# Hybrid attention and delta-rule layer: two groups of the triangular substitution side by side during the fourth head, two projection steps among the merges

## The chip, the cores and the metric

The kernel runs on one core of a Trainium2 chip, as one program. The metric is the device time of one execution in microseconds (us). The kernel before was timed in three runs; one more execution was recorded by the hardware profiler, and every line of a profile below comes from it.

## The reference, cut to what matters

The layer mixes 1024 latent tokens and 256 context tokens of width 1024 in two head groups: neighbourhood attention (8 heads) and a gated delta rule run in both directions (4 heads of 128, chunks of 64). The part that the change touches is the chunk's triangular inverse in the delta rule.

```python
    decay = jnp.exp(jnp.where(incl, gc[..., :, None] - gc[..., None, :], -jnp.inf))
    kb = k * beta[..., None]
    a = jnp.where(pos[:, None] > pos[None, :],
                  jnp.einsum('nbhid,nbhjd->nbhij', kb, k) * decay, 0.0)
    eye = jnp.eye(GDN_CHUNK, dtype=a.dtype)
    t_inv = lax.linalg.triangular_solve(eye + a, jnp.broadcast_to(eye, a.shape),
                                        left_side=True, lower=True, unit_diagonal=True)
    u = jnp.einsum('nbhij,nbhje->nbhie', t_inv, v * beta[..., None])
    w = jnp.einsum('nbhij,nbhjd->nbhid', t_inv, kb * jnp.exp(gc)[..., None])
```

The kernel inverts the 32 x 32 diagonal blocks by back substitution and puts the chunk's inverse together from them by small matmuls (the merge).

## The kernel before, in words

The work goes through these stages.

- `phase0` loads and modulates the tokens and starts the first projections.
- `phase2` goes through the four delta heads h = 0 to 3. Each head takes the steps Q, K (projection and short convolution of q and k), then F of the head before (`delta_front`: Gram products `pk`, decay `em`, the matrices `pm` and `qe`), then the steps `R V p p T p p U B`: R is a part of the residual gate (`res_gate`, it ends in the small matmul `pg` behind ScalarE's copy `growg`), V the projection and convolution of v (`acc_v`, `xp_v`), p one step of a filling generator, T the transposes to token order with the norms' squares and the rotary product (`tp`, `tok`, `rot`), U the transposes of v (`vtp`), B the transposes back (`tb`, `kq`).
- The filling generator `projections` has 32 steps; a step is 24 matmuls for one tile of a projection (`pz`, `pq`, `pk`) or 48 shorter ones for two tiles of values (`pv`). 16 of them are taken in `phase2`.
- `phase_a2` takes the other steps and lets two generators run beside them, by credits that each step adds: `blocks` (group 2 of the substitution, then loads for attention) and `merges` (`inv_merge` of the four heads, in the order of the table MERGES: matmuls `tz`, `tu` between copies on ScalarE and VectorE).
- `phase_b` holds attention and the scan of the delta rule, `phase4` the output projection.

The substitution works on 320 blocks of 32 x 32, one in each partition: `delta_front` gathers 80 of a head into `ab_dram`, and groups 0, 1 and 2 hold 120, 120 and 80 of them (`inv_load`). `inv_blocks` clears `vb`, sets its diagonal to 1 on GpSimd, and runs 31 pairs of VectorE instructions, an outer product into `tb` (L1078) and a subtraction from `vb` (L1081). The result goes to `yd`, from which the merges load. Group 0 is spread over the steps of h = 2 and the Q and K of h = 3, group 1 over the steps of h = 3, group 2 runs in `phase_a2`.

The order of the instructions on each engine is fixed when the program is built, by a scheduler that goes by priorities and estimated times; each engine then takes its instructions in that order. SyncE and ScalarE issue the transfers, each in its own order. All names in the rows (`acc_v2`) carry the head's number behind the name.

## Time and profile before

| what | value |
| --- | --- |
| median of 3 runs | 873.86 us (870.09 to 876.51) |
| span of the profiled execution | 869.9 us |
| the profiled execution's own time | not given apart from its span; the lowest timed run is 0.2 us above that span |
| instructions | 16461 |
| TensorE busy | 824.9 us, 95% |
| VectorE busy | 502.7 us, 58% |
| ScalarE busy | 417.3 us, 48% |
| GpSimd busy | 357.3 us, 41% |

The page gives busy time by engine over the span. Since TensorE is busy nearly always, a share over the whole span says little here; the waits of TensorE in each stage and its granted clock say more. In the views PE is TensorE's matmul, PEld its weight load, DVE VectorE, ACT ScalarE, POOL GpSimd, SP SyncE, and a `q` behind an engine means its instruction queue.

### The profile page before, as it was taken

Reading aid. Unit: us, or ns where it says so; the run is one execution under the profiler, and the core shown is the slowest. Engines: PE = TensorE matmul, PEld = TensorE weight load, DVE = VectorE, ACT = ScalarE, POOL = GpSimd, SP = SyncE. Lnnn points to the kernel's source line nnn. Section 1 sums busy time; section 2 is a strip of 40 time slices with the busy share of each in tenths; the row PEclk is TensorE's granted clock in tenths of the full one; section 3 lists DMA queues with packets and bytes.
Section 4 is the critical chain, followed back from the end, with each engine's and each line's share of the span. In section 5 each row is a group of like instructions: output and inputs, shape, how many; then the busy total and the mean of one; then the engine's idle time right before and its main releaser. Section 6 shows DMA issues by size and latency. Waiting matters only on the chain.

```text
span 869.9 us, 16461 instructions
## 1 busy us (share of the span) xinstructions
PE 824.9 (95%) x6082; PEld 696.4 (80%) x6082; DVE 502.7 (58%) x1051; ACT 417.3 (48%) x1087; POOL 357.3 (41%) x430
## 2 busy tenths in 40 slices
PE   6999999999999989989898999899999999999996
PEld 3678887888788867769786788788898988878885
DVE  3444455536743699859935964456666655653342
ACT  5244334753664643355314334366666667734210
POOL 2224141453462553328262100655757559624110
PEclk9999999999999999989998999699999999999999
DMA  8778352255444825562597569995967925134251
GB/s 340 265 259 295 97 170 88 73 170 168 142 157 154 221 85 170 176 171 81 176 283 226 160 187 290 419 258 149 313 179 262 259 78 191 49 110 133 87 184 69
DMA packets 86054, 159.65 MB, mean 184 GB/s; under 512 B 18373, under 2 KB 45334, under 8 KB 83798
## 3 DMA queue, kind: packets, MB, share of 16 engines
q1 hardware_dynamic: 78486, 144.94, 53.0%
q10 hardware_dynamic: 7488, 13.67, 5.1%
q8 instruction: 48, 0.79, 0.4%
q14 instruction: 32, 0.26, 0.1%
HBM read 109.51 MB, written 52.42 MB: 186 GB/s over the span
## 4 chain that ended last, share of the span: by engine, by line
PE 59%; DVE 16%; DMA 15%; issue 4%; ACT 2%; POOL 2%; SPq 1%; DVEq 0%; POOLq 0%; ACTq 0%
PE py L1369 3%; PE py L1370 3%; PE py L1371 3%; DVE tb L1078 3%; DVE vb L1081 3%; PE pa L1260 2%; PE pz L463 2%; PE pz L468 2%; PE pz L467 2%; PE po L789 2%; DMA wada<-in_w_ada 2%; PE pa L1271 2%; PE po L784 2%; DMA pm_dram<-pm 2%; PE tr L772 2%
## 5 line engine op out<-in xcount | busy, mean ns | idle before, releaser
L759 ACT ACTIVATE pt<-pt,nm 128x544 f32<-128x544 f32 (+1 forms) x64 | 50.5, 790 | 37.5 <-DVE nm L758 37.0
L758 DVE CUSTOM_DVE_ANT_0 pt<-sc,gm 128x544 f32<-128x544 f32 (+1 forms) x64 | 49.4, 771 | 32.2 <-PE sc L754 25.8
L742 POOL TENSOR_TENSOR gm<-gt,mk 128x288 f32<-128x288 f32 (+1 forms) x48 | 46.5, 971 | 29.1 <-DVE nm L758 28.8
L1232 POOL TENSOR_SCALAR kd<-kt,kd 128x128 f32<-128x128 f32 x72 | 42.7, 605 | 20.5 <-PE pa L1271 19.9
L1020 ACT ACTIVATE em<-em,gc 128x128 f32<-128x128 f32 x80 | 25.5, 391 | 34.9 <-DMA em<-gc_dram 29.7
L467 PE MATMUL pz<-hl,wh_gz 128*128 128x512 f32 x96 | 38.6, 402 | 0.0
L463 PE MATMUL pz<-hh,wh_gz 128*128 128x512 f32 x96 | 38.3, 399 | 0.0
L468 PE MATMUL pz<-hh,wl_gz 128*128 128x512 f32 x96 | 38.2, 398 | 0.0
L476 PE MATMUL pv<-wh_nv,hh 128*128 128x264 f32 x128 | 35.5, 296 | 2.0 <-ACT hh L265 1.7
L477 PE MATMUL pv<-wh_nv,hl 128*128 128x264 f32 x128 | 36.8, 292 | 0.0
L1431 DVE TENSOR_TENSOR finv<-py,ggb 128x512 f32<-128x512 f32 x16 | 10.9, 689 | 43.2 <-ACT finv L1430 43.1
L478 PE MATMUL pv<-wl_nv,hh 128*128 128x264 f32 x128 | 35.6, 287 | 0.0
L1274 DVE SCALAR_TENSOR_TENSOR s<-s,egl,pa 128x128 f32<-128x128 f32 x64 | 19.6, 344 | 27.2 <-PE pa L1271 27.2
L1039 POOL TENSOR_SCALAR_AFFINE_SELECT qe<-qe 128x256 f32<-128x256 f32 x32 | 25.5, 800 | 24.1 <-DVE qe L1038 24.1
L887 DVE SCALAR_TENSOR_TENSOR acc_v<-xp_v,cols,acc_v 128x1282 f32<-128x1282 f32 x16 | 29.1, 1817 | 10.9 <-ACT acc_v L885 10.6
L1078 DVE TENSOR_TENSOR tb<-ab,vb 120x31 f32<-120x31 f32 (+15 forms) x62 | 30.2, 487 | 8.7 <-DMA ab<-ab_dram 7.1
L1137 POOL COPY tm<-ld 32x320 f32<-32x320 f32 x16 | 7.4, 464 | 65.0 <-DMA tm_dram<-tm 27.1
L1430 ACT ACTIVATE finv<-py 128x512 f32<-128x512 f32 x16 | 9.5, 597 | 48.6 <-PE py L1371 30.5
L1238 POOL TENSOR_SCALAR vb<-v,beta 128x128 f32<-128x128 f32 x40 | 24.2, 604 | 20.4 <-DVE y L1244 17.2
L772 PE MATMUL tr<-c,pt 128*96 128x128 f32 (+1 forms) x192 | 31.8, 275 | 0.0
L1035 DVE SCALAR_TENSOR_TENSOR pm<-pk,beta,em 128x128 f32<-128x128 f32 x80 | 23.5, 342 | 14.0 <-PE pk L1028 10.9
L770 ACT COPY tcx<-tc 128x256 f32<-128x256 f32 x64 | 23.4, 366 | 16.2 <-PE tc L768 15.8
(432 smaller groups left out, 2852.7 us busy)
## 6 DMA issues: line engine op xcount, KB each, us to landing
wada<-in_w_ada SPq DMA_DIRECT2D x16, 512.0 KB
em<-gc_dram SPq DMA_DIRECT2D x20, 256.0 KB
pm_dram<-pm SPq DMA_DIRECT2D x20, 256.0 KB
tm_dram<-tm SPq DMA_DIRECT2D x8, 640.0 KB
kk<-qk_dram SPq DMA_DIRECT2D x16, 320.0 KB
tm<-tm_dram SPq DMA_DIRECT2D x4, 1280.0 KB
kq_dram<-kq SPq DMA_DIRECT2D x4, 1152.0 KB
kq<-kq_dram SPq DMA_DIRECT2D x4, 1152.0 KB
```

The costliest lines, as they stand in the source:

```text
L463: r = nc.tensor.matmul(ps, wh, xh, start=(k == 0), stop=False)
L467: nc.tensor.matmul(ps, wh, xl, start=False, stop=False)
L468: nc.tensor.matmul(ps, wl, xh, start=False, stop=(k == KC - 1))
L476: nc.tensor.matmul(ps, xh, wh, start=(k == 0), stop=False)
L477: nc.tensor.matmul(ps, xl, wh, start=False, stop=False)
L478: nc.tensor.matmul(ps, xh, wl, start=False, stop=(k == KC - 1))
L742: r = nc.gpsimd.tensor_tensor(self.gm[hh][:, 384 - n:384].rearrange("p (n c r) -> p n c r", c=nco, r=4), gv, self.mk[:, mo:mo + n].rearran ...
L758: nc.vector.tensor_tensor_reduce(pt[:, 384 - n:], sc[:, 512 - n:768], gm[:, 384 - n:], -1.0, 3.0e38, ALU.add, ALU.min, nm)
L759: self.last_exp = nc.scalar.activation(pt[:, 384 - n:], pt[:, 384 - n:], AF.Exp, bias=nm, scale=-1.0, accum_out=sums[:, ct, hh:hh + 1]).in ...
L772: self.pe(nc.tensor.transpose(pl[:m, rc * P:(rc + 1) * P], pt[:, 384 + (rc - 3) * m:384 + (rc - 2) * m], self.ident))
L1078: nc.vector.tensor_tensor(t3, bc(ab[:, 0:m, m:m + 1], [r, m, n]), bc(vb[:, m:m + 1, m:], [r, m, n]), ALU.mult)
L1232: r = nc.gpsimd.tensor_scalar(kd[d], kt_[:, t, :], self.kd[:, h, d, t:t + 1], None, ALU.mult)
```

## The change: two groups in one run

Groups 0 and 1 are no longer run one after the other. A new function `inv_pairs` loads both into the halves of one tile of 2 x 1024 columns, cuts away all but the strict triangle on GpSimd, sets the diagonals to 1, and substitutes in place: 30 pairs of VectorE instructions, each over both groups. It starts at h = 3, behind F of head 2; during h = 2 there is no substitution. The sign is moved into `pm` (the factor is now minus beta, kept in `nsc` until the scan needs its own values there), so that the substitution adds and the merges copy where they negated. At h = 2 two of the four `p` are left out, so that 18 instead of 16 steps of the filling generator remain for `phase_a2`, and a step there gives the merges 1.5 credits instead of 3. The gate preparation takes its small tiles as parts of one buffer of the `tok` pool.

```diff
                 step(h - 1, "F") if h else step(h, "G")
-                if h > 1:
-                    blocks = self.inv_groups((h - 2,), lambda nm, n: cv.tile([P, n], F32, name=nm, tag=nm[:2]))
-                for c in "RVppTppUB":
+                if h == 3:
+                    blocks = self.inv_pairs(cv)
+                for c in ("RVppTppUB", "RVppTppUB", "RVpTpUB", "RVppTppUB")[h]:
                     step(h, c)
                     next(blocks, None)
...
+        tmp = vp.tile([P, 512], F32, name="gtmp", tag="tok", bufs=6)
+        part = lambda o: tmp[:, 80 * o:80 * o + 80].rearrange("p (h d t) -> p h d t", h=4, d=2)
...
-        nc.vector.tensor_scalar(fl(self.nsc), fl(self.egc), -1.0, None, ALU.mult)
-        nc.vector.tensor_tensor(self.nsc[:, :, 1, :], self.nsc[:, :, 1, :], beta[:, :, 1, :], ALU.mult)
+        nc.vector.tensor_scalar(fl(self.nsc), fl(beta), -1.0, None, ALU.mult)
...
-                    nc.vector.scalar_tensor_tensor(pm[:, d, t - t0, :], pk[:, t - t0, 0, :], self.beta[:, h, d, t:t + 1],
+                    nc.vector.scalar_tensor_tensor(pm[:, d, t - t0, :], pk[:, t - t0, 0, :], self.nsc[:, h, d, t:t + 1],
                                                    em[:, d, t - t0, :], ALU.mult, ALU.mult)
...
+    def inv_pairs(self, pool):
+        nc = self.nc
+        ab = pool.tile([P, 2 * S], F32, name="ab", tag="ab")
+        tb = pool.tile([P, 480], F32, name="tb", tag="tb")[:120]
+        for g in range(2):
+            w = self.inv_load(g, ab[:, S * g:S * g + S])
+            nc.gpsimd.affine_select(w, w, [[-1, 32], [1, 32]], ALU.is_gt, 0.0, base=0, channel_multiplier=0)
+        ab = ab[:120].rearrange("p (g a b) -> p g a b", g=2, a=32)
+        nc.gpsimd.memset(bass.AP(ab.tensor, ab.offset, [list(ab.ap[0]), [S, 2], [33, 32]]), 1.0)
+        yield
+        for m in range(30, 0, -1):
+            n = 31 - m
+            t3 = tb[:, :2 * m * n].rearrange("p (g a b) -> p g a b", g=2, a=m)
+            nc.vector.tensor_tensor(t3, bc(ab[:, :, 0:m, m:m + 1], [120, 2, m, n]), bc(ab[:, :, m:m + 1, m + 1:], [120, 2, m, n]),
+                                    ALU.mult)
+            nc.vector.tensor_tensor(ab[:, :, 0:m, m + 1:], ab[:, :, 0:m, m + 1:], t3, ALU.add)
+            if m % 3 == 0:
+                yield
+        yield
+        for g in range(2):
+            self.yd[g] = self.dp.tile([120, 32, 32], F32, name=f"yd{g}")
+            nc.sync.dma_start(self.yd[g], ab[:, g])
...
-                nc.vector.tensor_tensor(vb[:, 0:m, m:], vb[:, 0:m, m:], t3, ALU.subtract)
+                nc.vector.tensor_tensor(vb[:, 0:m, m:], vb[:, 0:m, m:], t3, ALU.add)
...
-                nc.vector.tensor_scalar(dst, pu[sc], -1.0, None, ALU.mult)
+                nc.vector.tensor_copy(dst, pu[sc])
...
         if h == 0:
+            fl = lambda t: t.rearrange("p h d t -> p (h d t)")
+            nc.vector.tensor_scalar(fl(self.nsc), fl(self.egc), -1.0, None, ALU.mult)
+            nc.vector.tensor_tensor(self.nsc[:, :, 1, :], self.nsc[:, :, 1, :], self.beta[:, :, 1, :], ALU.mult)
...
-                for i, (g, r) in enumerate(zip(gens, (3, 3))):
+                for i, (g, r) in enumerate(zip(gens, (3, 1.5))):
```

Where this moves instructions is seen in the fixed orders. First VectorE in the third head, at the convolution of v (`acc_v2`), before:

```order
L1078 TENSOR_TENSOR tb0_2755<-ab0_2752,vb0_2754 120x87
L887 SCALAR_TENSOR_TENSOR acc_v2_2769<-xp_v2_2768,cols_62,acc_v2_2769 128x1282
L1081 TENSOR_TENSOR vb0_2754<-vb0_2754,tb0_2755 120x29x3
L529 TENSOR_TENSOR sl_k12_2902<-pk1_2_2876,sh_k12_2901 128x256
L887 SCALAR_TENSOR_TENSOR acc_v2_2769<-xp_v2_2768,cols_62,acc_v2_2769 128x1282
L1078 TENSOR_TENSOR tb0_2755<-ab0_2752,vb0_2754 120x112
```

The same place now:

```order
L887 SCALAR_TENSOR_TENSOR acc_v2_2757<-xp_v2_2756,cols_62,acc_v2_2757 128x1282
L529 TENSOR_TENSOR sl_k12_2884<-pk1_2_2858,sh_k12_2883 128x256
L887 SCALAR_TENSOR_TENSOR acc_v2_2757<-xp_v2_2756,cols_62,acc_v2_2757 128x1282 x3
L529 TENSOR_TENSOR sl_k10_3004<-pk1_0_2978,sh_k10_3003 128x512
L889 SCALAR_TENSOR_TENSOR acc_v2_2757<-xp_v2_2756,acc_v2_2757 128x1282
```

The steps of group 0 between the taps of the convolution are gone. Second GpSimd, where F of head 2 begins (`qe2` is masked there), before:

```order
L449 TENSOR_TENSOR wl_gv3_4_3538<-wr_gv3_4_3536,wh_gv3_4_3537 128x512
L1071 MEMSET vb1_3528 120x1024
L1039 AFFINE_SELECT qe2_2_3418<-qe2_2_3418 128x256
L1072 MEMSET vb1_3528 120x32
L1039 AFFINE_SELECT qe2_2_3418<-qe2_2_3418 128x256
```

And now:

```order
L449 TENSOR_TENSOR wl_gv3_4_3391<-wr_gv3_4_3389,wh_gv3_4_3390 128x512
L1040 AFFINE_SELECT qe2_2_3268<-qe2_2_3268 128x256 x2
L1040 AFFINE_SELECT qe2_4_3290<-qe2_4_3290 128x256 x2
L1040 AFFINE_SELECT qe2_6_3312<-qe2_6_3312 128x256 x2
L1040 AFFINE_SELECT qe2_8_3334<-qe2_8_3334 128x256 x2
```

The clearing of group 1's `vb` no longer stands ahead of the masks. Third VectorE in the fourth head, behind the convolution of v, now (L1080 and L1082 are the two instructions of a pair; `wl_nv0` is the low part of the weights of the value projection, which the matmuls `pv` read):

```order
L889 SCALAR_TENSOR_TENSOR acc_v3_3396<-xp_v3_3395,acc_v3_3396 128x1282
L1080 TENSOR_TENSOR tb_3377<-ab_3376 120x216
L556 SCALAR_TENSOR_TENSOR st_z10_3561<-st_z10_3561,pz1_0_3536 128x512
L1082 TENSOR_TENSOR ab_3376<-ab_3376,tb_3377 120x2x27x4
L1080 TENSOR_TENSOR tb_3377<-ab_3376 120x260
L1082 TENSOR_TENSOR ab_3376<-ab_3376,tb_3377 120x2x26x5
L1080 TENSOR_TENSOR tb_3377<-ab_3376 120x300
L1082 TENSOR_TENSOR ab_3376<-ab_3376,tb_3377 120x2x25x6
L1080 TENSOR_TENSOR tb_3377<-ab_3376 120x336
L1082 TENSOR_TENSOR ab_3376<-ab_3376,tb_3377 120x2x24x7
L449 TENSOR_TENSOR wl_nv0_6_3721<-wr_nv0_6_3719,wh_nv0_6_3720 128x528
```

Before, this weight part stood ahead of the last tap of the convolution, behind six instructions of the substitution. The first tokens `tok3` of the head follow 16 instructions of the pair later.

More of the change, by code (lines that the diff above doesn't have):

```diff
@@ L955, in gate_prep @@
         gt = self.gates
-        T = lambda nm, pool=vp: pool.tile([P, 4, 2, 10], F32, name=nm)
+        T = lambda nm, pool: pool.tile([P, 4, 2, 10], F32, name=nm)
         cp = self.cp
         gv = lambda lo: gt[:, :, lo:lo + 8].rearrange("p t (d h) -> p h d t", d=2)
-        sm = vp.tile([P, 2, 4, 2], F32, name="sm")
+        tmp = vp.tile([P, 512], F32, name="gtmp", tag="tok", bufs=6)
+        part = lambda o: tmp[:, 80 * o:80 * o + 80].rearrange("p (h d t) -> p h d t", h=4, d=2)
+        sm = tmp[:, 480:496].rearrange("p (a h d) -> p a h d", a=2, h=4)
         sml = I["smalls"]
@@ L965, in gate_prep @@
         nc.vector.tensor_scalar(beta, beta, 0.5, 0.5, ALU.mult, ALU.add)
-        y, e, s_, z, q, g = T("gy"), T("ge"), T("gs"), T("gz"), T("gq"), T("gg_")
+        y, e, s_, z, q, g = (part(o) for o in range(6))
         fl = lambda t: t.rearrange("p h d t -> p (h d t)")
@@ L984, in gate_prep @@
         nc.vector.scalar_tensor_tensor(fl(y), fl(q), 2.0, fl(y), ALU.mult, ALU.add)
-        ea = vp.tile([P, 4, 2], F32, name="ea")
+        ea = tmp[:, 496:504].rearrange("p (h d) -> p h d", h=4)
         nc.scalar.activation(ea, sm[:, 0], AF.Exp)
@@ L1170, in inv_merge @@
                                  tile_position=(64, 64))
-            nc.vector.tensor_scalar(tm[0][A, t0:t0 + 5, B], pus[0][A, :5], -1.0, None, ALU.mult)
-            nc.vector.tensor_scalar(tm[1][B, t0:t0 + 5, A], pus[1][B, :5], -1.0, None, ALU.mult)
+            nc.vector.tensor_copy(tm[0][A, t0:t0 + 5, B], pus[0][A, :5])
+            nc.vector.tensor_copy(tm[1][B, t0:t0 + 5, A], pus[1][B, :5])
         for d in range(2):
```

## The prediction

> **What bounds the kernel now.** I began with the page's first lines. TensorE is busy in 95% of the span, so only two things can give time back: stretches in which it waits, and stretches in which it runs at a lower granted clock.
>
> ```profile
> span 869.9 us, 16461 instructions
> PE 824.9 (95%) x6082; PEld 696.4 (80%) x6082; DVE 502.7 (58%) x1051; ACT 417.3 (48%) x1087; POOL 357.3 (41%) x430
> ```
>
> Second, busy time by stage. I cut the span where the program repeats itself: at the residual-gate matmul `pg` of heads 1, 2 and 3 (225.2, 297.3 and 375.0 us), at the last Gram product of head 3 (439.8) and at the first attention score (552.4). The columns are length, then busy time of PE, PEld, DVE, ACT and POOL, clock, DMA share, GB/s.
>
> ```profile
> 225.20:297.30 72.10, 72.10 (x373) 59.33 (x372) 39.16 (x58) 39.03 (x100) 33.22 (x34) 1.00 0.53 164
> 297.30:375.00 77.70, 69.61 (x365) 56.95 (x365) 67.06 (x120) 36.45 (x95) 30.76 (x34) 0.97 0.50 151
> 375.00:439.80 64.80, 61.79 (x393) 55.68 (x394) 53.33 (x104) 29.15 (x82) 30.64 (x23) 0.95 0.50 150
> 439.80:552.40 112.60, 104.17 (x1414) 86.87 (x1412) 63.71 (x136) 39.30 (x84) 28.30 (x41) 0.91 0.79 239
> ```
>
> The first row is head 1 to head 2's gate: no substitution runs, and TensorE never pauses. The second is the same code one head later with group 0 on VectorE: DVE rises from 39 to 67 us and TensorE loses 8 us. Third, the waits of TensorE in the second, third and fourth stretch, in that order (total, times, longest):
>
> ```profile
> PE tp L909 <- ACT sq L915: 3.3, 1, 3.3
> PE pg L427 <- ACT growg L421: 2.9, 1, 2.9
> PE tb L944 <- DVE tok L921: 1.4, 1, 1.4
> ...
> PE tb L944 <- DVE tok L921: 2.9, 1, 2.9
> ...
> PE tu L1167 <- DVE tm L1171: 2.1, 1, 2.1
> PE tz L1128 <- DVE ld L1116: 1.6, 1, 1.6
> PE pq L463 <- DVE sl_k L529: 1.6, 1, 1.6
> ```
>
> Fourth, the stretches in which the granted clock is halved (same columns as above). Each follows a wait, and costs half of its PE time:
>
> ```profile
> 319.60:323.00 3.40, 3.08 (x11) 2.58 (x12) 3.37 (x4) 3.24 (x16) 2.54 (x4) 0.50 0.19 73
> 374.20:381.00 6.80, 6.03 (x14) 4.11 (x15) 4.28 (x6) 5.22 (x13) 1.87 (x2) 0.50 0.78 182
> 469.80:476.60 6.80, 6.80 (x90) 5.67 (x84) 5.11 (x8) 6.61 (x15) 4.08 (x6) 0.50 0.74 257
> 497.10:500.50 3.40, 3.40 (x16) 3.24 (x16) 3.02 (x9) 2.13 (x5) 0.00 (x0) 0.50 0.91 340
> ```
>
> **The change, part by part.** I sum against the profiled span of 869.9 us; the median of the runs, 873.86, lies 4.0 above it, and I carry the difference over.
>
> *VectorE work.* A step's price comes from three groups of like shape (mean ns at the end of the busy part):
>
> ```profile
> L932 DVE TENSOR_TENSOR tok<-tok,rope 128x512 f32<-128x512 f32 x8 | 5.1, 683 | 0.0
> L931 DVE TENSOR_TENSOR rot<-tok,rope 128x512 f32<-128x512 f32 x8 | 5.1, 682 | 0.0
> ...
> L1081 DVE TENSOR_TENSOR vb<-vb,tb 120x256 f32<-120x256 f32 x2 | 0.8, 422 | 0.0
> ```
>
> From 256 to 512 elements is 0.26 us, so 1.02 ns an element and 0.16 us fixed. The old two groups are 4 x 31 = 124 instructions on 4 x 5456 elements: 20 + 22 = 42 us undisturbed (59.6 us measured, from the two rows of `tb` below). The new run is 60 instructions on 2 x 9920 elements: 9.7 + 20.2 = 30 us. That two groups in one access pattern cost no more per element is not shown for this operation; the near row is L931, which reads with a swapped half and a broadcast and costs what L932 does. I take equal rates; twice the rate per element would add 20 us (a rival below). DVE itself is not the bound, so these 12 us count only through the waits.
>
> ```profile
> 297.30:375.00 77.70, 2.48 (x18) 2.07 (x18) 30.30 (x62) 2.50 (x5) 0.97 0.50 151
> 375.00:439.80 64.80, 2.77 (x18) 2.13 (x18) 29.26 (x62) 2.61 (x5) 0.95 0.50 150
> ```
>
> *Third head (h = 2), substitution removed.* The 3.3 us wait is a chain that can be read in the timeline (start, length, instruction, idle before): VectorE steps L1078 and L1081 stand among the taps of `acc_v`, ScalarE sits 7.4 us in front of `xp_v`, and behind that stand the squares that free the transposes' PSUM.
>
> ```profile
> 310.25 1.36 DVE L1078 TENSOR_TENSOR tb<-ab,vb 120x112 f32<-120x112 f32 x1
> 311.53 2.59 DVE L887 SCALAR_TENSOR_TENSOR acc_v<-xp_v,cols,acc_v 128x1282 f32<-128x1282 f32 x1
> ...
> 317.94 1.27 ACT L888 ACTIVATE xp_v<-acc_v 128x1282 f32<-128x1282 f32 x1 [7.44 <-DVE acc_v L887]
> ```
>
> The new order has no step there and puts the squares ahead of `xp_v`. The 2.9 us wait starts from the same group: its result leaves at 360 us, GpSimd waits for that transfer before it may clear `vb` for group 1, the masks of `qe` stand behind the clearing, their transfers ahead of the next `em` load on SyncE's queue, and ScalarE copies `growg` only behind that `em`.
>
> ```profile
> 365.06 0.95 POOL L1071 MEMSET vb<- 120x1024 f32 x1 [3.56 <-DMA yd<-vb]
> 365.96 0.41 POOL L1039 TENSOR_SCALAR_AFFINE_SELECT qe<-qe 128x256 f32<-128x256 f32 x1
> ...
> 372.72 1.28 ACT L1020 ACTIVATE em<-em,gc 128x128 f32<-128x128 f32 x4 [3.53 <-DMA em<-gc_dram]
> ...
> 374.56 0.35 ACT L421 COPY growg<-parg 128x256 f32<-128x256 f32 x1
> ```
>
> Both links go. I count 3.3 + 2.9 + 1.4 us of waits, and half of the 3.08 and 6.03 us at half clock, 4.5: 12.1 us. What is late next is the key normalisation: transposes, squares, root, `tok`, then `tb`. Between its transposes and `tb` stand the 48 matmuls of `gpl_q`, some 11 us, the cover that head 1 has; I leave 1 us for small waits. **Net -11.1.** The two projection steps that no longer stand here (48 matmuls) cost nothing by leaving, since they are executed later; one step of 24 takes 5.6 us by its first and the next tile's first row:
>
> ```profile
> 302.63 0.40 PE L463 MATMUL pk<-hh,wh_nk 128*128 128x512 f32 x1
> ...
> 308.22 1.04 PE L909 MATMUL tp<-c,acc_q 128*128 128x128 f32 x8
> ```
>
> *Fourth head (h = 3), both groups.* I time this from `pg`. In the head before, group 0's block landed 8.3 us behind it:
>
> ```profile
> 297.32 0.59 PE L427 MATMUL pg<-growg,c 128*1 128x256 f32 x2
> ...
> 305.66 0.21 DVE L1078 TENSOR_TENSOR tb<-ab,vb 120x31 f32<-120x31 f32 x1 [3.35 <-DMA ab<-ab_dram]
> ```
>
> Now group 1's block lands at +8.3. A select over 1024 elements follows on GpSimd (by 0.41 us for 256 and 0.95 for a 1024 clearing: between 0.95 and 1.7, I take 1.5), then a weight split of 1.3 us stands ahead of the diagonal, so the pair starts at about +11.4. The taps of `acc_v` and `xp_v` end at some +18; then GpSimd's rotations of the query tiles begin. Beside them a two-input VectorE step takes a GpSimd operation's length, not its own: 1.36 us above, against 0.27 for the same form alone. The rows after it are a weight split, and the start of the rotations of this head with VectorE's steps beside them and behind them:
>
> ```profile
> 357.25 0.27 DVE L1078 TENSOR_TENSOR tb<-ab,vb 120x112 f32<-120x112 f32 x1
> ...
> 360.20 1.30 POOL L449 TENSOR_TENSOR wl_gv<-wr_gv,wh_gv 128x512 fp32r<-128x512 f32 x1 [1.21 <-ACT wh_gv L448]
> ...
> 395.23 1.74 POOL L931 TENSOR_TENSOR rot<-tok,rope 128x512 f32<-128x512 f32 x1 [8.17 <-ACT tok L912]
> ...
> 397.13 1.34 DVE L1078 TENSOR_TENSOR tb<-ab,vb 120x135 f32<-120x135 f32 x1
> 398.50 1.27 DVE L1081 TENSOR_TENSOR vb<-vb,tb 120x135 f32<-120x135 f32 x1
> ...
> 408.07 0.40 DVE L1078 TENSOR_TENSOR tb<-ab,vb 120x231 f32<-120x231 f32 x1
> ```
>
> In the new VectorE order the second split of the weights of the value projection, `wl_nv0_6`, stands behind eight more steps than today. At 1.3 us beside GpSimd for most of these eight, and 2.6 for the last tap ahead of them, it comes at about +29.5. TensorE, with 8 matmuls, three steps of 5.6 us, ten transposes and 20 short matmuls in front, wants it at about +25: a wait of 4.5 us. I add 0.8 us at the key transposes, which wait for squares, and 2.5 us of half clock after the long one (between 1.5 and 3.4 in the rows above). `tok` of this head now stands behind 30 steps of the pair, some 11 us further, at about +41; with that delay TensorE is at `tb` by +45, so the old 2.9 us wait goes. **Net 7.8 - 2.9 = +4.9.** If GpSimd does not hold the steps this is -2.9, if it holds all of them +16.
>
> The Trainium skill, "GPSIMD Engine Reference" (Key points), says that GpSimd shares its SBUF interfaces with VectorE and contends with instructions that have two SBUF inputs. The trace agrees (1.36 us against 0.27), and the rule speaks against a change that puts larger two-input steps beside the rotations; without it the 4.5 us would vanish and the sum would be about 7 us better, clock included.
>
> *Merges.* 18 projection steps instead of 16 remain for this stage, and the credit per step halves, so TensorE has about 30 more large matmuls, 7 us by the step above, between the first merge and the last. That covers the 2.1 us wait at `tu` and the half clock behind it (1.7 us of 3.4); I take 3 of the 3.8. The waits before the first merge (1.6 + 1.6, and 3.4 of half clock) stay: group 0's result is now written together with group 1's, at the end of the fourth head, and its small loads queue behind that write, about as late against TensorE as today. The tail behind the last projection (a chain of `tz`, `tu` and copies) keeps its length. **Net -3.0**, between -8 and +4.
>
> *The rest at nothing.* Negations that turn into copies read the same PSUM tiles in the same count; one multiplication of `nsc` fewer in the preparation and two small ones later, 0.2 to 0.6 us each on VectorE, stand where TensorE does not wait; the scratch tile of the preparation comes from a pool whose buffers nobody holds at that time; the attention and scan behind 552 us keep their order.
>
> Sum: -11.1 + 4.9 - 3.0 = -9.2 us, so 860.7 us of span and **864.7 us** of median.
>
> The Trainium skill, "TensorE: Matmul & The Clock Gate" (What's actually happening), lets the clock drop after an idle window of about 3.4 us. The rows differ: 2.9 us of waiting at 375 us was followed by 6.8 us at half clock, the 2.9 us at 417 us by none. By the page only the 4.5 us wait could cost clock, one window, 1.7 instead of 2.5, which moves the sum by 0.8.
>
> **Rivals.** (1) *GpSimd hardly holds the pair.* The new steps are longer, so fewer starts collide, and the weight split is in time. Then the fourth head has no wait: 7.8 us better, 857 us. For: behind the rotations the old steps ran undisturbed (0.40 us at 408). Against: beside the rotations, from 395 to 405 us, most were stretched like the two rows above. Chance 0.27. (2) *The cover is missed.* With 11 us less projection work in the third head, TensorE meets the key chain or the `em` loads earlier and waits there anyway, 3.3 + 1.4 us and their clock come back: 871 us. For: `em` loads wait for buffers that VectorE frees. Against: head 1 without a wait. Chance 0.23. (3) *Slower: the pair's access pattern costs twice per element.* Then the steps take 50 us, 20 more; of these 10 fall ahead of `tok` (6 us of wait and 3.4 us of clock) and 10 ahead of the last Gram products, whose PSUM waits for `pm` behind the pair (9 us and 3.4): +22, so 886 us. It decides from about 1.4 times the rate, where the gain is used up. Against it speaks L931. Chance 0.08. (4) Forecast: 0.42.
>
> **Numbers.** My forecast's own spread is 860 to 869. The range for 8 in 10 takes in rivals 1 and 2 with a few us of their own: 853 to 875; rival 3 is left out. A measurement of this kernel can tell about 1% (8.7 us). Faster by over 1% means below 865.1: rival 1 and just over half of the forecast, 0.50; within 1%: the other half and rival 2, 0.42; slower 0.08.
>
> **What would show it.** In the profile after: no wait of `tp` on squares and of `pg` on `growg` in the third head, VectorE below 45 us there; about 60 steps with some 480 elements at 0.65 us alone and 1.3 beside rotations; a wait of the value matmuls L478 on `wl_nv` of VectorE in the fourth head; no 2 us wait of `tu` on `tm`. Wrong if the pair's steps cost over 0.9 us alone, if `tb` waits longer than before, or if the first merge waits more than 4 us for `ld`.

## The result, and the profile after

The changed kernel takes **862.16 us** (median of 4 runs, 861.74 to 863.78) against 873.23 us (870.09 to 876.51) for the kernel before, timed beside it: a ratio of 0.9878, interval 0.9855 to 0.9902. It is faster by 1.2%. The forecast was 864.7 us of 873.86, a ratio of 0.9895, inside that interval. The profiled execution took 863.78 us, of which 862.1 are the span. Span against span the gain is 7.8 us, and by the medians it is 11.1: the execution profiled before was one of that kernel's shorter ones, the one profiled now the longest of its four.

The page of the changed kernel begins so:

```profile
span 862.1 us, 16412 instructions
PE 821.5 (95%) x6082; PEld 694.3 (81%) x6082; DVE 491.5 (57%) x988; ACT 418.0 (48%) x1087; POOL 362.6 (42%) x429
```

Busy time by stage, cut at the same places as before: `pg` of heads 1, 2 and 3, the last Gram product, the first attention score, the end. The last three rows are the half-clock stretches behind 350 us. Columns as in the prediction.

```profile
224.10:296.20 72.10, 72.10 (x373) 59.34 (x372) 39.09 (x58) 39.50 (x102) 33.43 (x34) 1.00 0.52 164
296.20:356.10 59.90, 58.81 (x326) 48.47 (x326) 41.76 (x56) 35.77 (x95) 33.37 (x31) 1.00 0.57 176
356.10:422.90 66.80, 60.07 (x383) 54.93 (x383) 56.19 (x88) 27.06 (x76) 28.60 (x21) 0.95 0.41 126
422.90:542.80 119.90, 113.19 (x1465) 92.59 (x1463) 73.87 (x151) 42.08 (x89) 34.00 (x47) 0.95 0.80 236
542.80:862.10 319.30, 302.12 (x2369) 265.44 (x2368) 170.27 (x463) 166.86 (x490) 157.99 (x214) 0.98 0.57 179
386.70:393.50 6.80, 5.76 (x26) 5.76 (x27) 6.56 (x12) 3.13 (x16) 6.80 (x4) 0.50 0.31 97
458.40:465.20 6.80, 6.68 (x47) 4.93 (x40) 5.52 (x7) 5.16 (x12) 2.20 (x4) 0.50 0.97 302
536.90:550.50 13.60, 12.66 (x93) 11.77 (x91) 5.18 (x12) 5.07 (x14) 8.39 (x15) 0.50 1.00 392
```

By length the stages changed by -17.8 us (third head), +2.0 (fourth), +7.3 (merges) and +1.8 (attention and scan); 1.1 us more went before head 1, where the two programs hardly differ. About 11 us of matmuls (48 of 0.23 us) moved from the heads to the merges, so lengths alone mislead: by the counts above 39 left the third head, 10 the fourth, and 51 came to the merges. The waits of TensorE from the third head's `pg` to the first score (total, times, longest):

```profile
PE pv L478 <- DVE wl_nv L449: 4.9, 1, 4.9
PE tz L1152 <- DVE ld L1140: 4.0, 1, 4.0
PE tp L909 <- ACT sq L915: 1.4, 2, 0.8
...
PE tb L944 <- DVE tok L933: 0.7, 1, 0.7
```

The waits of the third head on `sq`, `growg` and `tok` have shrunk to 0.7 us on `tok` (and 0.3 at `vtp`). The first row is the new wait that was foreseen; the third is the fourth head's. The second was 1.6 us before.

### The profile page after: what moved, and what is told of

It is laid out like the page before. It is cut to its first block, busy times and chain, and to the rows that moved or that the text cites. A ratio compares the mean times of both kernels' runs of the same rounds, so it can differ in the third digit from the quotient of the medians.

```text
span 862.1 us, 16412 instructions
## 1 busy us (share of the span) xinstructions
PE 821.5 (95%) x6082; PEld 694.3 (81%) x6082; DVE 491.5 (57%) x988; ACT 418.0 (48%) x1087; POOL 362.6 (42%) x429
## 4 chain that ended last, share of the span: by engine, by line
PE 68%; DMA 12%; DVE 10%; issue 4%; POOL 3%; ACT 2%; SPq 1%; DVEq 0%; POOLq 0%; ACTq 0%
PE py L1396 3%; PE py L1398 3%; PE py L1397 3%; PE pa L1287 3%; PE pz L463 3%; PE pz L467 3%; PE pz L468 3%; PE po L789 2%; PE pa L1298 2%; DMA wada<-in_w_ada 2%; PE tr L772 2%; PE po L784 2%; PE sc L754 2%; PE pv L478 2%; PE pv L476 2%
## 5 line engine op out<-in xcount | busy, mean ns | idle before, releaser
L1040 POOL TENSOR_SCALAR_AFFINE_SELECT qe<-qe 128x256 f32<-128x256 f32 x32 | 28.4, 887 | 42.6 <-DVE qe L1039 42.6
L478 PE MATMUL pv<-wl_nv,hh 128*128 128x264 f32 x128 | 37.5, 300 | 5.3 <-DVE wl_nv L449 4.9
L1036 DVE SCALAR_TENSOR_TENSOR pm<-pk,nsc,em 128x128 f32<-128x128 f32 x80 | 23.6, 344 | 19.6 <-PE pk L1029 16.2
L772 PE MATMUL tr<-c,pt 128*96 128x128 f32 (+1 forms) x192 | 32.1, 277 | 0.0
L449 POOL TENSOR_TENSOR wl_gz<-wr_gz,wh_gz 128x512 fp32r<-128x512 f32 x12 | 16.3, 1355 | 36.2 <-ACT wh_gz L448 34.8
L478 PEld LDWEIGHTS pv<-wl_nv,hh 128*128 128x128 f32 x128 | 25.2, 199 | 6.8 <-DVE wl_nv L449 5.1
```

The source lines that it names most:

```text
L478: nc.tensor.matmul(ps, xh, wl, start=False, stop=(k == KC - 1))
L772: self.pe(nc.tensor.transpose(pl[:m, rc * P:(rc + 1) * P], pt[:, 384 + (rc - 3) * m:384 + (rc - 2) * m], self.ident))
```

## The experiments

Unless said otherwise an edit is made on the changed kernel. Ratios are to the kernel before, run on the same chip; the changed kernel's is 0.9878. Each trace is of one execution, and not always of a typical one. `pg` of head 0, ahead of all that is compared here, begins between 145.6 and 152.3 us in these traces (147.5 in the changed kernel's), so where places in time are compared between runs, the distance from that `pg` is given too.

### Each half of the change alone

**Only the two projection steps and the credits**, on the kernel before:

```diff
-                for c in "RVppTppUB":
+                for c in ("RVppTppUB", "RVppTppUB", "RVpTpUB", "RVppTppUB")[h]:
...
-                for i, (g, r) in enumerate(zip(gens, (3, 3))):
+                for i, (g, r) in enumerate(zip(gens, (3, 1.5))):
```

> The kernel before with only the moved projection steps: two p fewer in the third head, 18 steps for the merges, 1.5 credits a step; the substitution stays where it was. Theory (the gain comes from the substitution leaving the third head): VectorE keeps 67 us of work there while TensorE has 48 matmuls, 11.2 us, less to cover it, so the waits of tp, tb and pg in that head grow from 7.6 us to 12 or more; the merges give back some 3 us. Sum +2 to +9 us against before, 875 to 882 us. Rival (the moved steps carry the gain, by covering the merges): the third head's waits stay as they are and the time falls to 862 to 867 us.

878.13 us, 1.0072 (1.0037 to 1.0107): slower. The waits of that kernel, from the third head to the first scan products:

```profile
PE pv L478 <- DVE wl_nv L449: 6.9, 1, 6.9
PE pa L1260 <- DMA v<-vt_dram: 6.2, 1, 6.2
PE vtp L826 <- DVE acc_v L889: 5.4, 1, 5.4
```

With the old substitution between the taps, less matmul work in the third head only uncovers `acc_v`. The first row is in the fourth head: with the steps moved, TensorE waits for the weight split also without the pair (the split runs 32.1 us behind `pg` of that head here). The merges now end 3 us behind the last projection (18.3 before), and TensorE pays at the next place: the scan waits 6.2 us for its loads of `v`.

**Only the pair**, with the old steps and credits (the same two lines the other way round, on the changed kernel):

> The changed kernel with the steps put back: four p in the third head as before, 16 steps for the merges, 3 credits a step. Theory: the third head has no wait over 1 us and its clock stays full (-11 us), the fourth head keeps its wait of 4.9 us for wl_nv and the half clock behind it (+6), the merges are as before (0, or up to 3 us worse, since the first merge waits 4.0 us for ld in the changed kernel and has less cover here). Sum -5 to -2 us: 868 to 871 us. Rival (the moved steps carry the gain): no gain, 871 to 875 us, with waits of 2 us and more left in the third head.

897.62 us, 1.0289 (1.0246 to 1.0333), 27 us beyond the expectation. By length the heads went as foreseen, -10.3 and +5.0 us, and the third has no wait at all. The fourth does not wait for VectorE's split, which here runs 17.9 us behind `pg`, but 3.1 us for `tok` and this for GpSimd's part of the weights:

```profile
PE pv L478 <- POOL wl_nv L449: 1.8, 1, 1.8
```

So the wait comes with the moved steps, with either form of the substitution; the pair alone does not make it. The merges collapsed. The stretch from the last projection (521.9 us) to the first score (578.9), and the end of the longest wait in it, on VectorE:

```profile
521.90:578.90 57.00, 26.77 (x500) 24.82 (x500) 15.06 (x27) 10.20 (x24) 7.55 (x15) 0.53 0.86 281
```

```profile
572.79 0.48 DVE L1176 COPY tm<-tu 32x320 f32<-32x320 f32 x1 [17.15 <-DMA tm_dram<-tm]
```

TensorE is busy for less than half of these 57 us, at half clock. The projections are used up, the DMA engines are 86% busy, and `inv_merge` waits 17 us for its own store of `tm` before it may write the buffer again. SyncE issues the two stores between 554.5 and 558.0 us, some 15 us ahead of the copy; in the changed kernel a copy that waits for such stores starts 3.6 us behind them.

**The credits alone**: 3 instead of 1.5 in the changed kernel.

```diff
-                for i, (g, r) in enumerate(zip(gens, (3, 1.5))):
+                for i, (g, r) in enumerate(zip(gens, (3, 3))):
```

> The changed kernel with 3 credits a step for the merges instead of 1.5 (18 steps stay). The pair alone, with 16 steps at 3 credits, lost 35 us between the Gram products and the first score. Theory (cover: what it lacked are the 48 matmuls; the rate matters little): 862 to 869 us, a tail of 10 to 18 us. Rival (the rate: at 3 credits the merges run into their own data and the projections are used up early): 880 us and more, a tail of 40 us and more.

874.95 us, 1.0021 (0.9995 to 1.0046): 12.8 us slower than the changed kernel, and more than my theory gave. The trace is of the fastest of ten executions (869.52 us). The last projection ends at 521.7 us, the first score comes 27.9 us later, at a mean clock of 0.65. A step of the projections waits for VectorE, and the merges wait for a copy into `tm` on GpSimd, which itself waits for the store of `tm`:

```profile
PE tz L1185 <- POOL tm L1161: 6.7, 1, 6.7
PE pz L463 <- DVE sl_k L529: 6.6, 1, 6.6
```

```profile
543.57 1.97 POOL L1161 COPY tm<-ld 32x320 f32<-32x320 f32 x4 [21.52 <-DMA tm_dram<-tm]
```

So neither half is a gain by itself (+0.7% and +2.9%), and the whole gain hangs on the two together: the pair makes the heads shorter, the later projections and the slower credits keep TensorE supplied until the merges are done. Of the 35 us that the pair alone loses against the changed kernel, the moved steps regain 22.7 at the old credits, and the slower credits the other 12.8; the slower credits with the old steps were not tried.

**One instruction for each group**, 120 instead of 60, with the same elements:

```diff
-            nc.vector.tensor_tensor(t3, bc(ab[:, :, 0:m, m:m + 1], ...), bc(ab[:, :, m:m + 1, m + 1:], ...), ALU.mult)
-            nc.vector.tensor_tensor(ab[:, :, 0:m, m + 1:], ab[:, :, 0:m, m + 1:], t3, ALU.add)
+            for g in range(2):
+                nc.vector.tensor_tensor(t3[:, g], bc(ab[:, g, 0:m, m:m + 1], ...), bc(ab[:, g, m:m + 1, m + 1:], ...), ALU.mult)
+            for g in range(2):
+                nc.vector.tensor_tensor(ab[:, g, 0:m, m + 1:], ab[:, g, 0:m, m + 1:], t3[:, g], ALU.add)
```

> The changed kernel with one instruction per group instead of one for both: 120 instructions on as many elements in the fourth head. By 0.16 us for an instruction the steps take 9.6 us more, and each one that starts beside a rotation or a weight split of GpSimd takes its 1.3 to 1.5 us. Theory (instruction count is what side by side saves, and VectorE has no slack in the fourth head): the pair ends 8 to 14 us later (442 to 448 us), the wait for wl_nv grows from 4.9 to 7 to 10 us, and the time rises by 6 to 14 us to 868 to 876. Rival (VectorE's work there lies in the cover): 860 to 865 us.

872.47 us, 0.9981 (0.9959 to 1.0003): the gain is gone. (The trace is of the slowest of ten executions, 876.86 us.) The two groups of steps, first in the changed kernel, then here (sum, mean ns):

```profile
L1080 DVE TENSOR_TENSOR tb<-ab 120x60 f32<-120x60 f32 (+14 forms) x30 | 21.5, 717 | 2.2 <-POOL ab L1073 1.5
L1082 DVE TENSOR_TENSOR ab<-ab,tb 120x60 f32<-120x60 f32 (+14 forms) x30 | 19.1, 635 | 0.7
```

```profile
L1081 DVE TENSOR_TENSOR tb<-ab 120x30 f32<-120x30 f32 (+14 forms) x60 | 25.3, 455 | 2.4 <-POOL ab L1073 2.0
L1083 DVE TENSOR_TENSOR ab<-ab,tb 120x30 f32<-120x30 f32 (+14 forms) x60 | 23.2, 420 | 0.0
```

That is 48.5 against 40.6 us, 7.9 more where 60 fixed parts of 0.16 us are 9.6. But the time was lost elsewhere than I had thought: the fourth head is 66.8 us long, as in the changed kernel. Without the tie between the groups, the first two steps of group 0 need not wait for group 1 and were placed in the third head:

```profile
312.21 1.28 DVE L1081 TENSOR_TENSOR tb<-ab 120x30 f32<-120x30 f32 x1 [0.83 <-POOL ab L1073]
313.41 2.62 DVE L887 SCALAR_TENSOR_TENSOR acc_v<-xp_v,cols,acc_v 128x1282 f32<-128x1282 f32 x1
```

`vtp` then waits 4.1 us for `acc_v`, and the clock is halved for 6.8 us. Two small steps among the taps, and the third head takes 65.1 us instead of 59.9; the merges take 4.6 us more. This run does not price the fixed parts, since two things changed in it.

### The wait in the fourth head, taken away in three ways

My theory was that the 4.9 us wait on `wl_nv` and the half clock behind it cost the change 7 to 8 us, caused by GpSimd's rotations that hold the pair's steps.

**The weight split ahead of the pair's larger steps.** The step with m = 26 is placed behind `wl_nv0_6`, and the yields are regrouped.

```diff
-            nc.vector.tensor_tensor(t3, ..., ALU.mult)
+            r = nc.vector.tensor_tensor(t3, ..., ALU.mult); m == 26 and self.order(r, self.split)
-            if m % 3 == 0:
+            for _ in range({30: 1, 27: 4, 20: 1, 13: 1, 6: 1}.get(m, 0)):
                 yield
```

> The changed kernel with VectorE's split wl_nv0_6 ordered ahead of the pair's steps for m = 26 to 24 (six instructions, in the trace 380 to 387 us), which are issued later. Theory (the split's place behind stretched pair steps makes the 4.9 us wait and the 6.8 us of half clock behind it): the split ends at about 382 us instead of 387.7, the wait shrinks to under 1 us and the half clock there goes; the first merge's wait for ld grows by 0 to 3 us, since TensorE comes earlier. Sum -8 to -5 us against the changed kernel: 854 to 857 us. Rival (the value matmuls wait for something behind the split anyway, the cast or the weights' transfer): the wait stays over 3 us under another name, 861 to 863 us.

865.54 us, 0.9939 (0.9916 to 0.9963): some 0.6% slower than the changed kernel, and the two intervals do not meet. The trace does not show this in full, since the profiled execution, 861.73 us, is the fastest of five. The wait and its half clock are gone and the Gram products end at 415.1 us instead of 422.9 (from `pg` of head 0, 5.9 us earlier), but the first score comes only 0.9 us earlier (from that `pg`, 1.0 us later):

```profile
PE tz L1152 <- DVE ld L1140: 8.1, 1, 8.1
PE tz L1185 <- POOL tm L1161: 4.5, 2, 3.3
```

What was gained is now waited for at the first merge, which starts at 456.7 us, against 457.5, and in the tail, 24.1 us long instead of 9.3.

**The rotations of the fourth head's queries left out**, so that its result is another.

```diff
-                if t0:
+                if t0 and not (which and h == 3):
```

> The changed kernel without the rotary product of head 3's queries, six GpSimd operations of 1.4 to 1.5 us each between 376 and 387 us; the result isn't the reference's there. Theory (GpSimd's operations stretch the pair's steps and so make the split late): the steps of 260 to 336 elements take 0.40 to 0.50 us instead of 1.4, TensorE's wait for wl_nv falls from 4.9 to under 1 us and the half clock behind it goes, the Gram products end 6 to 8 us earlier; the whole time moves less, 857 to 863 us, since the merges wait longer for ld, as in the run with the split first. Rival (the steps are long of themselves there): they stay over 1 us and the wait stays.

862.99 us, 0.9896 (0.9865 to 0.9927). The pair's steps at the same place, to be set beside 1.38 and 1.45 us in the changed kernel (rows below):

```profile
379.25 0.43 DVE L1080 TENSOR_TENSOR tb<-ab 120x260 f32<-120x260 f32 x1
...
382.17 0.51 DVE L1080 TENSOR_TENSOR tb<-ab 120x336 f32<-120x336 f32 x1
```

That GpSimd stretches the steps threefold is shown by this, and the wait on `wl_nv` goes with it. The first merge starts at 449.7 us and the first score comes at 536.8, 6.0 earlier (from `pg` of head 0, 9.6 and 7.8 us earlier); from there to the end it takes 324.6 us instead of 319.3. The scan now waits:

```profile
PE pa L1287 <- POOL vb L1265: 2.6, 1, 2.6
PE pa L1287 <- DMA v<-vt_dram: 2.1, 1, 2.1
```

**The pair's steps left out.**

```diff
-            nc.vector.tensor_tensor(t3, bc(ab[:, :, 0:m, m:m + 1], ...), ..., ALU.mult)
-            nc.vector.tensor_tensor(ab[:, :, 0:m, m + 1:], ab[:, :, 0:m, m + 1:], t3, ALU.add)
```

> The changed kernel without the pair's 60 VectorE steps (loading, cutting, diagonals and storing stay, so what is stored isn't the inverse). It prices all that the pair costs in its new place. Theory: the wait of 4.9 us and its clock go (-8), the transposes' 1.4 us too, and the first merge's wait for ld (4.0 us and its clock) goes, since the block is written some 50 us earlier (-6): 846 to 850 us. Rival (VectorE's work in the fourth head lies beside TensorE's and costs nothing): 859 to 863 us.

863.20 us, 0.9907 (0.9874 to 0.9939): my theory missed by 13 us at least, and the rival, that the steps cost nothing in total, was right. All 40 us of VectorE work are gone, the Gram products end 12.6 us earlier and the first score comes at 534.1 us, 8.7 earlier (from `pg` of head 0, 11.9 and 8.0 us); the remainder then takes 328.8 us, 9.5 more. The wait that took most of it, and SyncE's queue ahead of it (a row of several issues includes the time between them; the second store of `st_z` leaves at 532.3 us):

```profile
PE pa L1284 <- DMA v<-vt_dram: 6.4, 1, 6.4
```

```profile
523.13 9.53 SPq L557 DMA_DIRECT2D z_dram<-st_z  x2
534.10 0.95 SPq L1195 DMA_DIRECT2D tm_dram<-tm  x2
...
536.11 1.14 SPq L156 DMA_DIRECT2D v<-vt_dram  x1
```

The first load of `v` is issued at 536.1 us, behind the last projection's store of `st_z` and the merge's stores; in the changed kernel it is issued at 535.78, and 7 us pass before the first score. The attention starts earlier here, the loads of the scan do not.

### What sets the first merge

Five more kernels ask what holds the first `tz` near 457 us in the version with the split first, and the tail in the kernel with the pair alone.

**The stores of `tm` on ScalarE instead of SyncE**, in the split-first version and in the kernel with the pair alone; the theory (Q) was that they stand too late in SyncE's queue.

```diff
-            nc.sync.dma_start(self.tm_dram[h][:, d], tm[d])
+            nc.scalar.dma_start(self.tm_dram[h][:, d], tm[d])
```

> The run with the split first, and the merges' eight stores of tm issued by ScalarE instead of SyncE. In the run with the split first TensorE was done with the Gram products 7.8 us earlier than in the changed kernel, yet the first score came only 0.9 us earlier: its tail (last projection to first score) was 24.1 us instead of 9.3. Theory Q (order on SyncE's queue): there the third merge's second store of tm stands behind the scan's first load of 1280 KB, and the copies of head 3 wait for that store; without that the tail falls to 10 to 16 us and the median from 865.5 to 855 to 860 us. Theory P (pace): the merges take 85 us from the first tz on whatever the queue, and the first tz is set by ld; then the median stays at 862 to 867 us.

> The run with the pair alone (old steps, old credits), and the merges' stores of tm issued by ScalarE. With the pair alone the third merge's stores stood behind the scan's loads on SyncE's queue, TensorE waited 18.7 us for xo, and 61 us ran at half clock. Theory Q: those waits go, the time falls from 897.6 us by 20 to 35, to 863 to 877 us, about the kernel before or a little better. Rival (what was lacking is cover: the 48 matmuls that the moved steps bring): it stays above 888 us.

869.59 us, 0.9974 (0.9956 to 0.9992), and 894.41 us, 1.0249 (1.021 to 1.0287). Theory Q falls: the first gained nothing (0.9939 without this edit) and the second regained only some 3 of its 35 us. The pair alone with this queue still waits in its tail:

```profile
PE tu L1191 <- ACT z L1186: 12.2, 2, 7.6
PE tz L1185 <- DVE xo L1176: 10.5, 3, 7.4
```

The Trainium skill, "DMA: Bandwidth & Descriptors" (Issuing engines are not separate DMA queues), says that transfers from any issuing engine run on the same 16 DMA engines and interleave. The run fits this: between 540 and 575 us the DMA engines were 82% busy, and the time fell by only 3 us.

**Head 3's gather in rows of 4 KB** instead of 2560 pieces of 128 bytes:

```diff
-            ... ab_dram ... [[32, 32], [1024, 20], [1, 32]] <- pm_dram ... [[20 * P, 32], [P, 20], [1, 32]]
+            ... ab_dram ... [[1024, 20], [1, 1024]] <- pm_dram ... [[1024, 20], [1, 1024]]      (h == 3)
```

> The run with the split first, where the gather of head 3's blocks (2560 pieces of 128 bytes) is replaced by copies of as many bytes in rows of 4 KB, so group 2 works on other numbers and the result isn't the reference's. Theory D (small pieces fill the DMA engines, busy 94 to 105% from the Gram products' end to the first merge, and hold up the vl loads behind them): vl lands 4 to 9 us earlier, the first merge's wait for ld of 8.1 us falls below 4, and the median falls by 3 to 10 us to 855 to 862. Rival (vl waits for its place in the queue or for something else): ld within 2 us of where it was, 863 to 867 us.

866.74 us, 0.9927 (0.99 to 0.9954); the first `tz` at 458.8 us, after a wait of 6.7. The small pieces are not the cause. (Group 2 works on other numbers here.)

**Group 2's steps left out**, in the split-first version (its loads and stores stay):

```diff
-        for m in range(31, 0, -1):
+        for m in range(31 if gs != (2,) else 0, 0, -1):
```

> The run with the split first, without the 62 VectorE steps of group 2 (loading, clearing and storing stay, so head 3's blocks aren't inverses). Theory G (in every run so far the first score came 41 to 50 us behind the end of group 2's steps, save where the projections ran out of slack, and those steps took 48 to 54 us for some 20 us of work; so the stretch from the Gram products to the first score is set by the chain gather, group 2, head 3's merge, and what TensorE gains ahead of it is lost there): the merges end soon after the projections, the first score comes at 522 to 530 us instead of 541.9, and the median falls from 865.5 to 848 to 857 us, if the scan's loads don't come late. Rival (the wait of the first merge for ld sets the pace, 85 us from there): first score within 4 us of 541.9, median 860 to 866 us.

863.39 us, 0.9872 (0.9827 to 0.9917); the first `tz` at 459.3 us. Group 2's VectorE work does not hold it either. It has a share in the tail, which is 11.0 us here and 24.1 with the split first: without the steps group 2's blocks leave for `yd` at 457.2 us, with them at 498.8.

**The first merge's loads on ScalarE** (`pmf` and `vl` of head 0), past SyncE's queue:

```diff
-            nc.sync.dma_start(vl[32 * b:32 * b + 20], ...)
+            (nc.sync if h else nc.scalar).dma_start(vl[32 * b:32 * b + 20], ...)
```

> The run with the split first, where the six loads of the first merge (its two of pm and four of vl) are issued by ScalarE instead of SyncE, on whose queue they stood behind six stores of the attention's q and k and the load of group 2. In the runs with the pair and 18 steps the first score came 81 to 92 us behind the first tz, mostly 85 to 87, and the first tz 20 to 27 us behind the pair's end. Theory P (pace: the pair's end, the way to ld, and then four merges one behind the other set the first score): vl lands 6 to 10 us earlier, the wait for ld falls from 8.1 to 0 to 3 us, the first tz comes at 448 to 452 us instead of 456.7, the first score at 533 to 539 instead of 541.9, and the median falls from 865.5 to 857 to 862 us. Rival F (a floor of TensorE's own work and of the scan's loads; the changed kernel, the split first, the pair without steps, the run without the rotation and the one without group 2's steps all had spans of 860 to 863 us): what the merges gain, the scan's start loses, and the median stays at 862 to 867 us.

875.31 us, 1.0065 (1.0046 to 1.0084): slower than before the change, though the trace is of the fastest of six executions (871.26 us). ScalarE's six issues (shortest, median and longest in ns, then the first and last start) and VectorE behind them:

```profile
L1119 ACTq DMA_DIRECT2D pmf<-pm_dram x2: 317/679/1041, 433.1 to 440.6; - x2
L1130 ACTq DMA_DIRECT2D vl<-yd x4: 279/291/515, 441.0 to 448.7; - x4
```

```profile
449.73 0.69 DVE L529 TENSOR_TENSOR sl_k<-pk,sh_k 128x512 fp32r<-128x512 f32 x1 [16.13 <-ACT sh_k L527]
```

The issues themselves took 0.28 to 1.04 us each, but ScalarE waited ahead of most of them, so that the six took from 433.1 to 449.0 us, and its copies, on which VectorE and TensorE wait, stood behind. The last `vl` left at 448.7 us, later than by SyncE (440.6 with the split first), and the first `tz` stayed at 458.9 us. So the theory behind it was not tested.

The start of the first merge, between 456.7 and 459.3 us in the changed kernel and the split-first kernels (from `pg` of head 0, 310.0 to 312.3 us), looks like one limit, but the traces show two. In the changed kernel VectorE's transposes `vx`, `vd` and `ld` start as soon as `vl` has landed, at 453.96 us, and `ld` follows at 456.58. With the split first the loads land 4.5 us sooner:

```profile
449.49 1.25 DVE L1138 STREAM_TRANSPOSE vx<-vl 128x1024 f32<-128x1024 f32 x1 [8.80 <-DMA vl<-yd]
...
455.22 0.69 DVE L529 TENSOR_TENSOR sl_k<-pk,sh_k 128x512 fp32r<-128x512 f32 x1 [3.11 <-ACT sh_k L527]
455.83 0.83 DVE L1140 STREAM_TRANSPOSE ld<-vd 128x640 f32<-128x640 f32 x1
```

`vd` is done at 452.0 us, but in VectorE's fixed order `sl_k` of a projection now stands ahead of `ld`, and waits for ScalarE's `sh_k`, which starts only at 454.59 us, behind the issue of a weight load at 454.14. The other split-first traces on SyncE's loads have the same idle time ahead of `sl_k` (2.2 to 2.8 us); without the rotations no `sl_k` stands there, and the first merge starts at 449.7 us. No run puts `ld` ahead of `sl_k`, so what this place is worth is not known.

When the loads land stays open. From their issue to `vx` some 8 to 10 us pass in the changed kernel and with the split first, and the DMA engines are nearly full meanwhile; in the changed kernel:

```profile
446.00:452.00 6.00, 6.00 (x28) 4.88 (x27) 1.48 (x5) 0.67 (x2) 1.30 (x1) 1.00 1.03 222
```

That this traffic as a whole sets the landing is likely, not what a run showed.

## Why the prediction was right, and where it was wrong

**Third head, -11.1: right.** TensorE's idle time there went from 8.1 to 1.1 us and the 4.5 us of half clock went: -11.5. The cover held, with 0.7 us at `tb`; rival 2 did not happen. (Most of the half clock of 374.2 to 381.0 us lay, by the table, in the fourth stage; the prediction counts it here, and so does this sum.) Cause and place were shown by the run with the pair alone, whose third head has no wait, by the run with the moved steps alone, where the old substitution among the taps keeps a wait of 5.4 us, and by the run with one instruction for each group, where two steps there brought back 4.1 us and a half clock.

**Fourth head, +4.9: mechanism right, size 1.7 short.** Idle time went from 3.0 to 6.7 us, and half of the 5.76 us at half clock is 2.9: +6.6. The rows of VectorE that carry it:

```profile
367.93 1.34 DVE L1080 TENSOR_TENSOR tb<-ab 120x60 f32<-120x60 f32 x1 [1.53 <-POOL ab L1073]
...
379.23 1.38 DVE L1080 TENSOR_TENSOR tb<-ab 120x260 f32<-120x260 f32 x1
...
385.57 1.45 DVE L1082 TENSOR_TENSOR ab<-ab,tb 120x336 f32<-120x336 f32 x1
386.95 0.74 DVE L449 TENSOR_TENSOR wl_nv<-wr_nv,wh_nv 128x528 fp32r<-128x528 f32 x1
...
397.08 0.66 DVE L1080 TENSOR_TENSOR tb<-ab 120x480 f32<-120x480 f32 x1
398.35 1.02 DVE L921 TENSOR_TENSOR tok<-tp,rq_y_g 128x256 f32<-128x256 f32 x2
```

From `pg` at 356.1 us: the pair starts at +11.8 (forecast 11.4), the split comes at +30.9 (29.5), `tok` at +42.3 (41), and the old `tb` wait is gone, each as worked out. The 0.66 us at 480 elements, where 0.65 was computed, refutes rival 3. Rival 1 is refuted too: the rotations did hold the steps. The rule of the Trainium skill, "GPSIMD Engine Reference" (Key points), on inputs that GpSimd and VectorE share, weighed ahead of the result as speaking against the change, held at this place (1.38 us against 0.43). What failed is the sentence beside it, that without the rule the sum would be some 7 us better: split first, no rotations and no steps at all each took the wait away, and none is faster than the changed kernel. Nor is the wait the pair's alone: the moved steps alone have it (6.9 us), the pair alone does not.

**Merges, -3.0: the sum right in part by luck, its parts wrong.** The stage grew by 7.3 us and took 11 us of matmuls, -3.7. But I had the waits before the first merge stay at 1.6 us; the one on `ld` is 4.0, at the bound that I had named for being wrong, and 6.8 us of half clock follow. And "the tail keeps its length" was the step that failed most: from the last projection to the first score it went from 18.3 to 9.3 us. The tail before, then now:

```profile
534.10:552.40 18.30, 15.17 (x341) 13.93 (x341) 7.00 (x14) 6.52 (x16) 5.38 (x10) 0.70 0.97 341
```

```profile
533.50:542.80 9.30, 8.38 (x202) 8.09 (x201) 4.98 (x10) 2.28 (x5) 5.41 (x10) 0.68 0.85 297
```

I had priced the moved steps and credits by one wait of 2 us. By the run with 3 credits the slower credit alone is worth 12.8 us here, and by the run with the pair alone the pair without both is 35 us slower. The moved projections are cover for a chain of merges that waits for transfers; the profile of before showed it, with a clock of 0.70 and DMA engines 97% busy in its tail, and I read that as a constant. The prediction's list of half-clock stretches leaves out the longest one, which begins in this tail:

```profile
541.50:558.50 17.00, 13.79 (x104) 12.43 (x101) 5.58 (x14) 4.10 (x10) 10.32 (x17) 0.50 1.02 420
```

**The rest at nothing: +1.8 -1.1.** The half clock that begins at 536.9 us reaches 7.7 us into the scan stage (6.1 before), and the waits of the scan on `y` of VectorE add up to 4.4 us (3.0 before). The 1.1 us before head 1 are in the range in which `pg` of head 0 moves between profiles of these programs (145.6 to 152.3 us).

**The offset.** The span came out at 862.1 us where 860.7 was forecast; the 4.0 us that I added for the median do not exist as a constant, since here an execution's own time lies 1.7 above its span and this execution was the slowest of its four. Both slips stay under 0.5%.

The sum thus described what the two traces differ by, within 1.4 us. It did not describe what each term is worth. Kernels whose Gram products end 6 to 13 us earlier than the changed one's (from `pg` of head 0) come out no faster, because something else is next: with the split first, VectorE's order at the first merge and the tail; without the rotations or the steps, whose merges start at 449.7 and 437.7 us and end early, the first loads of the scan.

No version that computes everything beat the changed kernel.

## What to carry to other kernels

Where several stages are each near a limit of their own, a removed wait is worth what the next limit leaves of it: look for the next thing that cannot start earlier, here a transfer or an instruction in another engine's fixed order, before a wait is priced. Work that fills TensorE is a resource to be placed; moving it can be worth more than the wait that the change was about, and a tail at half clock with full DMA engines says that it lacks. Try each half of a compound change alone: here both were slower than the kernel before. And when several runs stop at the same time, look in each trace for what they stop at: here it was not the same thing.

## What the runs showed of the hardware

Not every GpSimd instruction holds VectorE. Here is GpSimd beside the rows above, two forms in the changed kernel:

```profile
383.68 2.97 POOL L933 TENSOR_TENSOR tok<-tok,rot 128x512 f32<-128x512 f32 x2
386.62 5.71 POOL L170 TENSOR_TENSOR rq_y_rho<-rq_y_rho,mhalf 128x32 f32<-128x32 f32 x1
```

And VectorE beside the second:

```profile
390.43 0.60 DVE L1080 TENSOR_TENSOR tb<-ab 120x420 f32<-120x420 f32 x1
```

Beside the first (1.5 us each) the steps took 1.45 us; beside the second, a power of 5.7 us on 32 columns with two inputs, they took the undisturbed price.

The half clock behind a wait need not be of the wait's length: it lasted 6.8 us behind 4.9 and behind 4.0 us, and the last spell above lasted 13.6 us. The Trainium skill, "TensorE: Matmul & The Clock Gate" (What's actually happening), has a window of about 3.4 us; the lengths here are near multiples of it, twice one window behind each of the two waits, so the single window that I worked out from it was too little.

Transfers issued by ScalarE can stop its computing for longer than the issues take: the six in the last experiment took 0.28 to 1.04 us each, and VectorE waited 16.1 us for the copy behind them.
